# A routed expert's down product as one plain float32 product instead of three split ones

## The chip, the core and the metric

The kernel runs on one core of one Trainium2 chip. The metric is the time of one execution on the device in microseconds (us). Three timed runs of the kernel before gave 2541.50, 2541.91 and 2543.68, so the median is 2541.91.

The engines are named as the profile names them: PE is the matrix engine (PEld its weight loads), DVE the vector engine, ACT the scalar engine, POOL the engine that here only issues indirect DMAs (gathers and scatters), and SP the engine whose queue issues the weight loads. SPq, ACTq and POOLq are these engines' queues. PEclk is the clock granted to PE as a share of its full speed.

## The reference, cut to what matters

The program is one layer with attention and a mixture of experts, followed by two further layers with a dense feed-forward. Everything is float32. The change touches the experts alone. There are 512 tokens of width 1024 and 64 experts with an inner width of 256; each token goes to 8 experts.

```python
def swiglu(x, w1, w3, w2):
    return (jax.nn.silu(x @ w1) * (x @ w3)) @ w2

def expert_block(args):
    e, toks, gs = args
    xb = t[toks]                                     # gather of up to 128 token rows
    return swiglu(xb, w1[e], w3[e], w2[e]) * gs[:, None]

routed = jax.ops.segment_sum(out, row_tok, num_segments=n_tok)
```

For one expert, w1 and w3 are 1024 x 256 and w2 is 256 x 1024: 1 MB each, so 3 MB for every expert.

## The kernel before, in words

**How float32 is multiplied.** A weight tile of 128 x 2048 float32 is split in two (`_K.split`, lines 217 to 224): ACT copies it to a reduced float32 type (`wh`, line 220) and DVE subtracts that copy from the raw tile (`wl`, line 221). The activations are split in the same way (`xet` for the tokens, `aet` for the inner activations). A product is then three matmuls, low by high, high by low, high by high (`_K.mm3`, lines 226 to 230). The adaptive-norm weights at the start of the program are the one place where PE multiplies raw float32 tiles (line 547).

**The weight stream.** `_Stream` (lines 71 to 178) holds a list of jobs, each a load of a raw tile (`wraw`, issued on SP at lines 110 and 112) and a flag that says whether the tile is split. `get` hands out the next job: it loads ahead up to `raw` jobs (`LR`, 8 in the expert loop), splits ahead up to `ahead` jobs (`LA`, 2), and returns the two halves, or the raw tile itself where the flag is false.

**The slots.** All large tiles come from one pool of 22 slots of 8 KB a partition (`slot`, line 198): raw tiles, `wh`, `wl`, `xet`, and the expert's output `eo`, two of which share a slot. A slot is given out again when its last user is done, the one that came free first being taken first. Who takes a slot waits for its last user, on whichever engine.

**The experts.** The 64 experts are ordered by how many tokens they have (`moe_units`, line 965). The first 32 run alone, three of them with a second block of rows; the last 32 run in pairs that share one block of 128 rows, 64 for each. So there are 67 down products in all. `moe_ops` sets the order of work: up of one expert, down of the expert before it, and so on. An up takes two jobs (half of w1 and w3 each, 24 matmuls on PE together), a down takes one (w2, 12 matmuls). Between them stand the transposes of the next tokens (`xet<-xg`, line 233) and of the inner activations (`act_t`, line 1398). A down's result is scaled by the gates into `eo`, one half by DVE (line 1415) and one by ACT (line 1413). POOL then adds it to `acc` in DRAM by an indirect DMA (line 1217). Each of these scatters waits until the one before has landed. A loop for overflowing experts (line 1552) stands behind the last expert; it has no turn in the profiled execution, but all engines meet at it.

The order on every engine is that of the program text. The last expert jobs are followed in the stream by the weights of the next layer (`plan_mla`, line 1713).

Of the kernel before, what the change touches and what calls it, by code (L numbers as in the profile page):

```python
# [11 lines left out]
F32 = mybir.dt.float32  # L12
F32R = mybir.dt.float32r
BF16 = mybir.dt.bfloat16
I32 = mybir.dt.int32
AF = mybir.ActivationFunctionType
# [16 lines left out]
FIX, PAIRS = 2, 16  # L33

CAPS = ((2, 128), (5, 192), (16, 128), (24, 96), (32, 80), (50, 64), (64, 48))
LR=8; LA=2; MOE_RAW=7
MORE=(5,6)
NR=3; RQ=3; RV=2
NF=7
# [141 lines left out]
class _K:  # L181
# [806 lines left out]
    def plan_moe(self):  # L988
        a = self.a
        kp = lambda w, k: w.rearrange("(k p) n -> p k n", k=k)  # L990
        wr, s1, s3 = kp(a["w_router"][0], 8), kp(a["ws1"][0], 8), kp(a["ws3"][0], 8)
        j = [([wr, s1[:, :, 0:128]], True), ([s1[:, :, 128:256], s3[:, :, 0:128]], True),
             (s3[:, :, 128:256], True)]
        units = self.moe_units()
        regs = {}

        def weight(nms, k, r, ks):
            def f():
                if r < FIX:
                    v = [a[nm][0, r].rearrange("(p k) n -> p k n", k=k)[:, ks] for nm in nms]  # L1000
                else:
                    if r not in regs:
                        regs[r] = self.nc.sync.value_load(self.perm[0:1, r:r + 1], min_val=0, max_val=NE - 1)
                    v = [a[nm][0, bass.ds(regs[r], 1)].rearrange("e (p k) n -> p (e k) n", k=k)[:, ks] for nm in nms]
                return v if len(v) > 1 else v[0]
            return f() if r < FIX else f
        ops = self.moe_ops()
        for i, (op, u, m) in enumerate(ops):
            r = units[u][0][m]
            if op == "up":  # L1010
                j += [(weight(("w1", "w3"), 8, r, slice(4 * h, 4 * h + 4)), True) for h in range(2)]
                if i == 1:
                    j.append((kp(a["ws2"][0], 2), True))
            else:
                j.append((weight(("w2",), 2, r, slice(0, 2)), True))
        return j

    def moe_begin(self, hT):
# [67 lines left out]
    def moe_block(self, hT, h2d, x1d):  # L1086
        nc, V, a, st = self.nc, self.nc.vector, self.a, self.st
# [128 lines left out]
        def scatter(o, idx):  # L1216
            nc.gpsimd.indirect_dma_start(out=acc, out_offset=IndirectOffsetOnAxis(ap=idx, axis=0),  # L1217
                                         in_=o, in_offset=None, compute_op=OP.add)
# [158 lines left out]
        def xpose(x):  # L1377
            t = self.slot(F32R, "xet")
            xv = x.rearrange("p (d k) -> p k d", k=8)
            for j in range(2):  # L1380
                self.trs(t[:, j * 512:j * 512 + 512].rearrange("p (a b) -> p a b", b=128),
                         t[:, 1024 + j * 512:1536 + j * 512].rearrange("p (a b) -> p a b", b=128),
                         [xv[:, 4 * j + i] for i in range(4)])
            r = lambda t: t.rearrange("p (a b) -> p a b", b=128)
            return r(t[:, :1024]), r(t[:, 1024:])

        def up(ps, xT, w, half):

            o = ps.rearrange("p (m n) -> p m n", m=2)
            for kk in range(4):  # L1390
                kc = 4 * half + kk
                self.mm3(o, (xT[0][:, kc], xT[1][:, kc]), (w[0][:, :, kk], w[1][:, :, kk]), kc == 0, kc == 7)
# [4 lines left out]

        def act_t(sg):
            av = sg[:, 256:].rearrange("p (f k) -> p k f", k=2)
            t = self.small.tile([128, 512], F32R, name="aet", bufs=4)  # L1400
            r = lambda t: t.rearrange("p (a b) -> p a b", b=128)
            H, L = r(t[:, :256]), r(t[:, 256:])
            self.trs(H, L, [av[:, 0], av[:, 1]])
            return H, L

        def down(aT, w, gate, o, rows):
            for n in range(2):
                ps = self.ps()
                c = slice(n * 512, n * 512 + 512)
                for f in range(2):  # L1410
                    self.mm3(ps, (aT[0][:, f], aT[1][:, f]), (w[0][:, f, c], w[1][:, f, c]), f == 0, f == 1)
                if n:
                    nc.scalar.activation(o[rows, c], ps[rows], AF.Copy, scale=gate[rows])
                else:
                    V.tensor_scalar(o[rows, c], ps[rows], gate[rows], None, OP.mult)  # L1415
        first = [0]
        for _, nb in units:
            first.append(first[-1] + len(nb))
        st.raw, st.ahead = LR, LA
        ops = self.moe_ops()  # L1420
# [18 lines left out]
        def acts_t():  # L1439
            for u in ready:  # L1440
                aTs[u] = [act_t(sg) for sg in sgs.pop(u)]
            ready.clear()
# [57 lines left out]
        for i, (op, u, m) in enumerate(ops):  # L1500
# [13 lines left out]
            if op == "up":  # L1514
# [5 lines left out]
                w = st.get(True)  # L1520
# [4 lines left out]
                w = st.get(True)  # L1525
# [6 lines left out]
            else:  # L1532
                if u in ready:
                    acts_t()
                w = st.get()
                rows = slice(64 * m, 64 * m + 64) if len(ranks) > 1 else slice(0, 128)
                if m == 0:
                    outs[u] = []
                    for _ in nb:
                        if not half:  # L1540
                            t = self.slot(F32, "eo")
                            half.extend([t[:, 1024:], t[:, :1024]])
                        outs[u].append(half.pop())
                for b, n in enumerate(nb):
                    i = first[u] + b
                    down(aTs[u][b], w, gt[:, i:i + 1], outs[u][b], rows)
                    scatter(outs[u][b][rows][:n], (isc2 if m else isc)[:n, i:i + 1])
# [4 lines left out]
        with self.tc.For_i(0, nreg) as _:  # L1552
            ereg = nc.sync.value_load(li[0:1, 0:1], min_val=0, max_val=NE - 1)
            wt = []
            src = {nm: a[nm][0, bass.ds(ereg, 1)].rearrange("e (p k) n -> p (e k) n", k=k)
                   for nm, k in (("w1", 8), ("w3", 8), ("w2", 2))}
            for i in range(2):
                wv = self.slot(F32, f"ov_{i}")
# [4 lines left out]
            wv = self.slot(F32, "ov_w2")  # L1563
# [16 lines left out]
            ps = self.ps()  # L1580
# [8 lines left out]
            gt1 = self.sm([128, 1], "ov_gt", bufs=1)  # L1589
            c, cg = self.sm([128, 8, 3], "tc")[:, :1], self.sm([128, 8, 3], "tg")[:, :1]  # L1590
# [5 lines left out]
            xTe = xpose(xg(0))  # L1596

            H, L = self.slot(F32R, "wh"), self.slot(F32R, "wl")

            def wsplit(wv, how, **d):  # L1600
                self.split(H, L, wv)
                return H.rearrange(how, **d), L.rearrange(how, **d)
            ps = self.ps()
            for i in range(2):
                up(ps, xTe, wsplit(wt[i], "p (m k n) -> p m k n", m=2, n=256), i)
            sg = self.t2k("sg")
            act(sg, ps, slice(0, 128))
            aT = act_t(sg)
            o = wt[0][:, :1024]
            down(aT, wsplit(wt[2], "p (k n) -> p k n", k=2), gt1, o, slice(0, 128))  # L1610
            scatter(o, is1)
            l2 = self.t2k()[:, 0:3 * W + 3].rearrange("p (a b) -> p a b", b=W + 1)
            V.tensor_copy(l2, ll)
# [542 lines left out]
```

## Time and profile before

| | us |
|---|---|
| median of the timed runs | 2541.91 |
| the profiled execution, its own time | 2537.97 |
| its span, first to last instruction | 2536.2 |
| expert stage, from the first ups to the last down | 480 to 1215, 735 |
| PE busy in that stage | 667.51 |
| DVE busy in that stage | 620.79 |
| ACT busy in that stage | 488.03 |
| DMA engines busy in that stage | 0.96 of it, 324 GB/s |

The stage's numbers are from a view that gives each engine's busy time in a stretch. A matmul of 128 x 512 is recorded as busy for some 0.39 us but the next one starts 0.23 us after it, since matmuls are pipelined; so PE's pace is read from starts, not from durations. A DMA share is the mean over the core's 16 DMA engines, and can read a little over 1. Idle time that is ascribed to an engine which had long been done belongs to another cause, often a DMA.

### The profile page before, as it was taken

What the parts mean: (1) busy time and instruction counts of PE and PEld (TensorE: products, weight loads), DVE (VectorE), ACT (ScalarE), POOL (GpSimd) and SP (SyncE); (2) the same over time, 40 slices, a digit from 0 to 9 for tenths busy, and PEclk for the clock granted to TensorE, in tenths of its full rate; (3) what the DMA queues carried; (4) which work ended last, traced back from release to release, by engine and by line L of the source; (5) the groups of instructions that cost most, each with busy time, mean ns of one, the idle gap of its engine ahead of it and who ended that gap; (6) DMA issues with size and microseconds to landing.
All of it is one profiled execution on the core that took longest, in us unless ns stands there. A gap on an engine that the chain in (4) does not pass through costs nothing.

```text
span 2536.2 us, 30312 instructions
## 1 busy us (share of the span) xinstructions
PE 2308.6 (91%) x11356; PEld 1868.5 (74%) x11356; DVE 1604.4 (63%) x2569; ACT 1056.6 (42%) x1446; POOL 340.5 (13%) x184
## 2 busy tenths in 40 slices
PE   8877988798889899999599999999999998999998
PEld 4555767677767777777477788888788876888886
DVE  4599667697888888988576653333555667433335
ACT  2552433366657666777244222222234432322230
POOL 0642000133334323332100000000000000000000
PEclk9888999899989999999799999999999998999999
DMA  9443134699989999999311332332141121323310
GB/s 331 168 140 79 39 114 165 223 352 301 344 267 319 341 307 347 361 362 337 105 32 54 129 107 76 100 116 75 59 140 51 51 100 62 105 83 116 100 67 33
DMA packets 195014, 422.21 MB, mean 166 GB/s; under 512 B 21329, under 2 KB 99921, under 8 KB 186545
## 3 DMA queue, kind: packets, MB, share of 16 engines
q1 hardware_dynamic: 169984, 353.44, 39.8%
q0 software_dynamic: 12944, 39.20, 6.7%
q10 hardware_dynamic: 11938, 27.62, 3.0%
q8 instruction: 90, 1.47, 0.2%
q14 instruction: 58, 0.48, 0.1%
HBM read 390.78 MB, written 35.52 MB: 168 GB/s over the span
## 4 chain that ended last, share of the span: by engine, by line
PE 62%; DVE 20%; DMA 9%; ACT 4%; issue 4%; POOL 0%; ACTq 0%; DVEq 0%; SPq 0%; POOLq 0%
PE b L228 20%; PE b L229 19%; PE b L230 19%; DMA acc<-eo,isc 7%; DVE wl L221 6%; PE b L233 3%; ACT wh L220 2%; DVE work L754 1%; PE b L547 1%; DVE m L750 1%; DMA wraw<-in_w_ada_dram 1%; DVE ln_st L1643 1%; DVE work L732 1%; PE b L2029 1%; DVE eo L1415 1%
## 5 line engine op out<-in xcount | busy, mean ns | idle before, releaser
L221 DVE TENSOR_TENSOR wl<-wraw,wh 128x2048 fp32r<-128x2048 f32 (+2 forms) x311 | 701.7, 2264 | 397.5 <-ACT wh L220 328.9
L220 ACT ACTIVATE wh<-wraw 128x2048 fp32r<-128x2048 f32 (+2 forms) x311 | 584.4, 1887 | 181.0 <-DVE wl L221 62.1
L228 PE MATMUL b<-xtl,wh 128*128 128x512 f32 (+1 forms) x928 | 344.0, 371 | 2.9 <-DVE xtl L221 2.9
L229 PE MATMUL b<-xth,wl 128*128 128x512 f32 (+1 forms) x928 | 341.9, 368 | 0.0
L230 PE MATMUL b<-xth,wh 128*128 128x512 f32 (+1 forms) x928 | 341.8, 368 | 0.0
L228 PE MATMUL b<-wl,xet 128*128 128x512 f32 x536 | 222.4, 415 | 18.7 <-DVE wl L221 18.2
L1217 POOL DMA_INDIRECT acc<-eo,isc x67 | 155.2, 2316 | 485.0 <-DVE P L1151 123.5
L229 PE MATMUL b<-wh,xet 128*128 128x512 f32 x536 | 214.2, 400 | 2.2 <-DVE xet L221 2.2
L230 PE MATMUL b<-wh,xet 128*128 128x512 f32 x536 | 215.2, 401 | 0.0
L228 PEld LDWEIGHTS b<-xtl,wh 128*128 128x128 f32 x928 | 176.5, 190 | 32.7 <-DVE xtl L221 3.6
L230 PEld LDWEIGHTS b<-xth,wh 128*128 128x128 f32 x928 | 176.2, 190 | 28.8
L229 PEld LDWEIGHTS b<-xth,wl 128*128 128x128 f32 x928 | 176.4, 190 | 27.9
L228 PE MATMUL b<-wl,aet 128*128 128x512 f32 x268 | 117.1, 437 | 33.9 <-DVE wl L221 32.8
L228 PE MATMUL b<-wl,ath 128*128 128x512 f32 x352 | 139.3, 396 | 5.8 <-DVE wl L221 5.8
L230 PE MATMUL b<-wh,ath 128*128 128x512 f32 x352 | 138.6, 394 | 0.0
L229 PE MATMUL b<-wh,atl 128*128 128x512 f32 x352 | 138.6, 394 | 0.0
L926 ACT ACTIVATE p<-b,nm 128x128 f32<-128x128 f32 (+3 forms) x128 | 67.0, 526 | 166.2 <-DVE nm L923 127.1
L228 PEld LDWEIGHTS b<-wl,xet 128*128 128x128 f32 x536 | 104.0, 194 | 40.5 <-DVE wl L221 18.3
L230 PEld LDWEIGHTS b<-wh,xet 128*128 128x128 f32 x536 | 103.5, 193 | 23.6
L229 PEld LDWEIGHTS b<-wh,xet 128*128 128x128 f32 x536 | 103.9, 194 | 22.4 <-DVE xet L221 2.6
L229 PE MATMUL b<-wh,aet 128*128 128x512 f32 x268 | 113.0, 421 | 1.9 <-DVE aet L221 1.9
L230 PE MATMUL b<-wh,aet 128*128 128x512 f32 x268 | 111.1, 415 | 0.0
(461 smaller groups left out, 4342.0 us busy)
## 6 DMA issues: line engine op xcount, KB each, us to landing
wraw<-in_w_dram SPq DMA_DIRECT2D x256, 512.0 KB
wraw<-in_w_dram SPq DMA_DIRECT2D x64, 1024.0 KB
wraw<-in_ffn_w_gu_dram SPq DMA_DIRECT2D x44, 1024.0 KB
wraw<-in_w_ada_dram SPq DMA_DIRECT2D x24, 1024.0 KB
wraw<-in_ffn_w_down_dram SPq DMA_DIRECT2D x20, 1024.0 KB
wraw<-in_diff_w_in_dram SPq DMA_DIRECT2D x12, 1024.0 KB
wraw<-in_w_in_dram SPq DMA_DIRECT2D x8, 1024.0 KB
wraw<-in_w_in_dram SPq DMA_DIRECT2D x12, 512.0 KB
```

What stands on the lines that cost most here:

```text
L220: nc.scalar.activation(H, x, AF.Copy)
L221: nc.vector.tensor_tensor(out=L, in0=x, in1=H.bitcast(F32), op=OP.subtract)
L228: mm(ps, s[0], m[1], start=start, stop=False)
L229: mm(ps, s[1], m[0], start=False, stop=False)
L230: mm(ps, s[0], m[0], start=False, stop=stop)
L233: self.nc.tensor.transpose(ps, x, self.ident[:x.shape[0], :x.shape[0]])
L547: nc.tensor.matmul(ps, cb[:, kc, :], w[:, kk, :], start=False, stop=kc == 7)
L732: V.scalar_tensor_tensor(w, r[:, :nk], wi, w, op0=OP.mult, op1=OP.add)
L750: V.max(m8[qt - 1], work(qt))
L754: V.match_replace(work(qt), m8[qt - 1], work(qt), -3e38)
L926: nc.scalar.activation(p[:, :nk], ps[:, :nk], AF.Exp, bias=nm, accum_out=sm)
L1217: nc.gpsimd.indirect_dma_start(out=acc, out_offset=IndirectOffsetOnAxis(ap=idx, axis=0), in_=o, in_offset=None, compute_op=OP.add)
```

## The change

The jobs of w2 in the expert loop carry a false flag: the stream hands out the raw tile. `act_t` no longer splits the inner activations: it transposes into PSUM and ACT copies them once, as plain float32. `down` makes one plain float32 matmul of the raw tile for each of the four (column half, inner half) pairs, in place of three matmuls of split halves. `LR` is 9 in place of 8. The loop for overflowing experts is changed in the same way.

```diff
-LR=8; LA=2; MOE_RAW=7
+LR=9; LA=2; MOE_RAW=7
...
-                j.append((weight(("w2",), 2, r, slice(0, 2)), True))
+                j.append((weight(("w2",), 2, r, slice(0, 2)), None))
...
         def act_t(sg):
             av = sg[:, 256:].rearrange("p (f k) -> p k f", k=2)
-            t = self.small.tile([128, 512], F32R, name="aet", bufs=4)
-            r = lambda t: t.rearrange("p (a b) -> p a b", b=128)
-            H, L = r(t[:, :256]), r(t[:, 256:])
-            self.trs(H, L, [av[:, 0], av[:, 1]])
-            return H, L
+            t = self.small.tile([128, 256], F32, name="aet", bufs=4)
+            ps = self.ps()
+            for f in range(2):
+                self.tr(ps[:, f * 128:f * 128 + 128], av[:, f])
+            nc.scalar.activation(t, ps[:, :256], AF.Copy)
+            return t
...
                 for f in range(2):
-                    self.mm3(ps, (aT[0][:, f], aT[1][:, f]), (w[0][:, f, c], w[1][:, f, c]), f == 0, f == 1)
+                    nc.tensor.matmul(ps, aT[:, f * 128:f * 128 + 128], w[:, f, c], start=f == 0, stop=f == 1)
```

On PE, in the early part of the expert loop, stands before this: the transposes of the next tokens (`xg`), and then the down product of an expert (`wl` and `wh` are the halves of its w2, `aet` its activations), of whose twelve matmuls the first six are shown.

```order
L233 MATMUL b<-ident,xg 128x128 x8
L228 MATMUL b<-wl,aet 128x512
L229 MATMUL b<-wh,aet 128x512
L230 MATMUL b<-wh,aet 128x512
L228 MATMUL b<-wl,aet 128x512
L229 MATMUL b<-wh,aet 128x512
L230 MATMUL b<-wh,aet 128x512
```

And now, from the last matmul of the up before it to the token tables (`P`) behind it:

```order
L230 MATMUL b<-wh,xet 128x512
L233 MATMUL b<-ident,xg 128x128 x8
L1412 MATMUL b<-wraw,aet 128x512 x4
L1166 LDWEIGHTS P
L1166 MATMUL b<-idc,P 128x3
```

The twelve matmuls are four, at the same place in the order, and they read the raw tile.

On ACT, which copies the high halves, one pair of experts in the later part of the loop is this before (`xet` the next tokens, `sg` the inner activations, `eo` half of a down's result):

```order
L220 ACTIVATE wh<-wraw 128x2048 x2
L220 ACTIVATE xet<-b 128x512 x2
L1395 ACTIVATE sg<-b 64x256
L220 ACTIVATE wh<-wraw 128x2048
L1413 ACTIVATE eo<-b,gt 64x512
L220 ACTIVATE wh<-wraw 128x2048
L220 ACTIVATE aet<-b 128x256
L220 ACTIVATE wh<-wraw 128x2048
L1395 ACTIVATE sg<-b 64x256
L220 ACTIVATE wh<-wraw 128x2048
L1413 ACTIVATE eo<-b,gt 64x512
```

And now:

```order
L220 ACTIVATE wh<-wraw 128x2048
L220 ACTIVATE xet<-b 128x512 x2
L1395 ACTIVATE sg<-b 64x256
L220 ACTIVATE wh<-wraw 128x2048
L1414 ACTIVATE eo<-b,gt 64x512
L1404 ACTIVATE aet<-b 128x256
L220 ACTIVATE wh<-wraw 128x2048
L1395 ACTIVATE sg<-b 64x256
L220 ACTIVATE wh<-wraw 128x2048
L1414 ACTIVATE eo<-b,gt 64x512
```

Two of the pair's six copies are gone, and `aet` stands directly behind `eo`; on DVE the two `wl` that belong to them and `aet` are gone in the same way.

On SP, at the end of the expert loop, the loads of the next layer stand like this before, ahead of the overflow loop (`nov` is its count of turns):

```order
L110 DMA wraw<-in_mla_w_ukv_dram 128x512 x2
L110 DMA wraw<-in_mla_w_uq_dram 128x2x128 x3
L110 DMA wraw<-in_mla_w_ukv_dram 128x512 x2
L110 DMA wraw<-in_mla_w_uq_dram 128x2x128 x3
L110 DMA wraw<-in_mla_w_ukv_dram 128x512 x2
L1551 TENSOR_LOAD nov
```

And now:

```order
L110 DMA wraw<-in_mla_w_uq_dram 128x2x128 x3
L110 DMA wraw<-in_mla_w_ukv_dram 128x512 x2
L110 DMA wraw<-in_mla_w_uq_dram 128x2x128 x3
L110 DMA wraw<-in_mla_w_ukv_dram 128x512 x2
L1552 TENSOR_LOAD nov
```

One job of the next layer (three pieces of `w_uq` and two of `w_ukv`) stands behind the loop now, and behind the four loads of `acc` that follow it.

## Rows read from the trace of the kernel before

**Rows 1.** Busy time by stretch; the first row names the columns.

```profile
core 0: us, PE busy (x) PEld busy (x) DVE busy (x) ACT busy (x) POOL busy (x), PEclk, DMA share, GB/s
480.00:1215.00 735.00, 667.51 (x3290) 538.73 (x3291) 620.79 (x653) 488.03 (x476) 241.93 (x112) 0.95 0.96 324
1040.00:1160.00 120.00, 113.80 (x512) 90.69 (x510) 105.07 (x79) 91.34 (x80) 38.50 (x19) 1.00 1.02 365
610.00:620.00 10.00, 7.83 (x27) 6.34 (x28) 9.32 (x9) 6.08 (x8) 7.55 (x3) 0.62 0.63 122
740.00:750.00 10.00, 5.10 (x22) 3.70 (x22) 8.41 (x45) 0.00 (x0) 0.00 (x0) 0.52 0.37 91
```

**Rows 2.** Groups by line and form, 480 to 1215; busy and mean, then idle before.

```profile
L221 DVE TENSOR_TENSOR wl<-wraw,wh 128x2048 fp32r<-128x2048 f32 x191 | 435.4, 2287 | 89.2 <-ACT wh L220 63.0 <-issue 10.3 <-DMA acc<-eo,isc 5.7
...
L220 ACT ACTIVATE wh<-wraw 128x2048 fp32r<-128x2048 f32 x191 | 363.9, 1913 | 63.9 <-DMA acc<-eo,isc 48.4 <-DMA wraw<-in_w_dram 9.2 <-DMA x<-x1d 5.1
```

**Rows 3.** PE in order of time: two pairs of experts.

```profile
1024.31 1.04 PE L233 MATMUL b<-ident,xg 128*128 128x128 f32 x8
...
1063.15 1.04 PE L233 MATMUL b<-ident,xg 128*128 128x128 f32 x8
...
1081.33 1.04 PE L233 MATMUL b<-ident,xg 128*128 128x128 f32 x8
...
1084.00 0.50 PE L228 MATMUL b<-wl,aet 128*128 128x512 f32 x1 [1.63 <-DVE wl L221]
...
1086.90 0.40 PE L228 MATMUL b<-wl,xet 128*128 128x512 f32 x1
```

**Rows 4.** The plain products of line 547: order of time, then durations.

```profile
48.88 7.13 PE L547 MATMUL b<-wraw,g 128*128 128x512 f32 x16
...
L547 PE MATMUL b<-wraw,g x64: 592/592/1222, 7.7 to 55.4; 128*128 128x512 f32 x64
```

**Rows 5.** PE in order of time: stalls in the expert loop.

```profile
536.85 0.77 PE L228 MATMUL b<-wl,aet 128*128 128x512 f32 x1 [3.41 <-DVE wl L221]
...
612.17 0.80 PE L228 MATMUL b<-wl,xet 128*128 128x512 f32 x1 [7.87 <-DVE wl L221]
...
617.46 1.11 PE L233 MATMUL b<-ident,xg 128*128 128x128 f32 x8
...
1183.55 0.50 PE L228 MATMUL b<-wl,aet 128*128 128x512 f32 x1 [3.71 <-DVE wl L221]
```

**Rows 6.** The chain that ended last: what stood ahead of one stall.

```profile
596.24 11.41 DMA acc<-eo,isc
...
607.88 1.92 ACT wh L220
```

**Rows 7.** Waits, 480 to 1215: total, times, longest.

```profile
POOL acc L1217 <- DMA acc<-eo,isc: 114.5, 17, 10.4
...
ACT wh L220 <- DMA acc<-eo,isc: 48.4, 14, 7.2
...
ACT wh L220 <- DMA wraw<-in_w_dram: 9.2, 2, 8.7
```

**Rows 8.** Waits of SP's queue, 440 to 1215.

```profile
SPq L112 <- PE b L230: 165.6, 71, 12.4
```

**Rows 9.** POOL in order of time: scatters.

```profile
637.41 3.43 POOL L1217 DMA_INDIRECT acc<-eo,isc  x1 [6.89 <-DVE aet L221]
...
649.49 1.56 POOL L1217 DMA_INDIRECT acc<-eo,isc  x1 [5.47 <-DMA acc<-eo,isc]
...
1223.87 1.41 POOL L1217 DMA_INDIRECT acc<-eo,isc  x1 [4.55 <-DMA acc<-eo,isc]
```

**Rows 10.** Around the loop's end: ACT, then SP's loads, then ACT.

```profile
1215.94 0.69 ACT L1413 ACTIVATE eo<-b,gt 128x512 f32<-128x512 f32 x1 [3.48 <-PE b L230]
...
1267.32 1.41 SPq L110 DMA_DIRECT2D wraw<-in_mla_w_uq_dram  x3
...
1311.35 1.69 ACT L220 ACTIVATE wh<-wraw 128x1792 fp32r<-128x1792 f32 x1
```

More of the change, by code (lines that the diff above doesn't have):

```diff
@@ L1598, in moe_block @@
             H, L = self.slot(F32R, "wh"), self.slot(F32R, "wl")
-            def wsplit(wv, how, **d):
-                self.split(H, L, wv)
-                return H.rearrange(how, **d), L.rearrange(how, **d)
+            four = lambda t: t.rearrange("p (m k n) -> p m k n", m=2, n=256)
             ps = self.ps()
             for i in range(2):
-                up(ps, xTe, wsplit(wt[i], "p (m k n) -> p m k n", m=2, n=256), i)
+                self.split(H, L, wt[i])
+                up(ps, xTe, (four(H), four(L)), i)
             sg = self.t2k("sg")
@@ L1609, in moe_block @@
             o = wt[0][:, :1024]
-            down(aT, wsplit(wt[2], "p (k n) -> p k n", k=2), gt1, o, slice(0, 128))
+            down(aT, wt[2].rearrange("p (k n) -> p k n", k=2), gt1, o, slice(0, 128))
             scatter(o, is1)
```

## The prediction, made before the change was run

> **What bounds the kernel now.** I read the busy time by stretch first, since the change touches one stage only, the experts from 480 to 1215. Look there for what is nearly full: PE 667.5 of 735 us, DVE 620.8, the DMA engines at a share of 0.96 [rows 1]. Three things are close to full at once, so the sum has to be made against each of them.
>
> The DMA engines. In a smooth stretch, 1040 to 1160, their share reads 1.02; this is full. At that share the stage's transfers, which the change leaves as they are, would take 735 x 0.96 / 1.02 = 692 us. The DMA floor is thus 43 us under today's stage. Those 43 us are stretches such as 610 to 620 (share 0.63) and 740 to 750 (0.37) [rows 1].
>
> PE. The order of time shows its pace. Two pairs of experts take 1063.15 - 1024.31 = 38.8 us, 19.4 for a pair, while the next pair, from its transposes at 1063.15 to the next ones at 1081.33, runs with no real gap in 18.2 [rows 3]. So PE stands still for about 1.2 us in a pair, and the DMA engines, not PE, set the pair's pace.
>
> What makes PE stand still. At 612.17 an up has waited 7.87 us for a low half (`wl`) [rows 5]. The chain of waits says what is behind it: a scatter that took 11.41 us, then ACT's copy `wh` [rows 6]. ACT waited because the slot it had to write into was an `eo` that the scatter was still reading. ACT lost 48.4 us to such scatters in 14 waits, and 9.2 us to weights that had not landed [rows 7]. So the hold-ups come from slots, not from late loads. SP's loads too wait mainly for PE to give slots back, 165.6 us on line 230's matmuls alone [rows 8]. While PE stands, no slots come free, no loads start, and the DMA engines run dry: this is the share of 0.63 right behind the stall.
>
> **The change part by part.** The sum is made against the profiled execution (2537.97 us: a span of 2536.2 and 1.8 around it), which lies 3.9 under the median of the runs; differences carry over to that median.
>
> PE's products. A down has 12 matmuls, from 1084.00 to 1086.90, 2.90 us with a start-up of some 0.1, so 2.80 of pace [rows 3]. The plain product is in the trace with the same shape at line 547: 16 records, two passes for each of 8 products, in 7.13 us, the last of them 0.592 long [rows 4]. The pace is (7.13 - 0.592) / 15 = 0.436 us a pass, 0.872 a product. Four products are 3.49 us, against 2.80: +0.70 for a down. With 67 downs PE gets 47 us more work. A paired cycle without gaps grows from 18.2 to 19.6 us, which is 0.2 over today's 19.4: in the pairs PE becomes about as tight as the DMA engines are.
>
> The splits. 64 of the 192 splits of weight tiles go. DVE loses 64 x 2.287 = 146 us, ACT 64 x 1.913 = 122 [rows 2], and DVE also the low half of each `aet`. Neither engine is full, so none of this counts by itself; it counts where PE waited for `wl`, and there the cause was mostly a slot.
>
> The slots. A lone expert took three raw tiles, three `wh`, three `wl`, one `xet` and half an `eo`: 10.5 slots. Now it is 8.5. The pool of 22 goes round in 22 / 8.5 = 2.6 experts instead of 2.1; at 735 / 64 = 11.5 us for an expert, an `eo` is asked for again between 5 and 6 us later. That is near the size of the waits for scatters (48.4 / 14 = 3.5 us on average, 7.2 at most) [rows 7], so I expect most of them to go. What is late next is PE itself.
>
> PE's room. PE was idle for 735 - 667.5 = 67.5 us [rows 1]. Behind each long stall its clock is low as well: the up from 612.17 to 617.46 took 5.29 us in place of about 2.8, at a granted clock of 0.62 in that stretch [rows 1, 5]. I count 13 such places, the first at 536.85 and the last at 1183.55, with 1.7 to 2.5 us lost in each, some 24 us. Together 92 us are PE's to gain, and 735 - 92 + 47 = 690 is its new floor. Two losses do not hang on slots: the overflow tables around 740 to 750, where PE is busy for 5.10 of 10 us [rows 1], 5 us; and the last experts, where 3.71 us at 1183.55 [rows 5] and some 1.7 of slow matmuls behind it come from the loop running out, with an estimated 5 to 6 at the entry, where PE waits for the tables: 11 together. So PE's real floor is 706, above the DMA floor of 692.
>
> The ninth load is worth little: what holds a load back is a slot. Its bounds are 0 and the 3 us that 1 MB takes at 324 GB/s [rows 1]; I take 0. The `w2` raw tile is now held until its product is done, but two tiles fewer are held beside it.
>
> The loop's end. One job of the next layer moves on SP's queue past the overflow loop and the loads of `acc`. The next such job was issued at 1267.32 anyway, and the moved one is first wanted by ACT's copy at 1311.35 [rows 10]: 44 us of cover, so nothing. The last down is 0.7 us longer, but its scatter started at 1223.87, seven us behind the `eo` that it writes (1215.94 + 0.69), since scatters stand in line [rows 9, 10]: nothing again.
>
> The sum. Today's stage lies 43 us over its highest floor. With slots that come round a quarter later I keep 17 of the 43: 706 + 17 = 723, so 12 us less. With 5 to 25 kept, the forecast's own range is -24 to -4. On the profiled run it gives 2526, on the median **2530 us**.
>
> **A rule that is weighed.** For PE, the rows above show no gap in 18.2 of 19.4 us. The Trainium skill ("Perfetto Trace Analysis", Identifying the Most-Contended Engine) says to judge the matrix engine's room by the busy share of its weight loads rather than of its matmuls. By that rule 538.7 of 735 [rows 1], 73%, leaves more than a quarter free: the 47 us would cost nothing and the DMA floor would be the end, 43 us less. The rows speak against it: in a gapless stretch the starts set the pace. This is the last rival below.
>
> **The rivals.**
> *PE becomes the bound and the stalls stay (slower).* If PE's waits are not mostly slots, for instance because scatters simply take 11 to 12 us however many slots there are and `eo` piles up one expert later, then the idle stays and each down adds its 0.70 us. It decides at 47 of the 92 us: more idle left than that and the kernel is slower. With two thirds left (61 us) it is 14 us slower, 2556; with all, 47 slower. For it: pairs have only 1.2 us of idle to pay for 1.4. Against it: the waits of ACT for slots [rows 7], and DVE and ACT off the path.
> *The scatters set the pace (no change).* Scatters run one behind another: 637.41 to 649.49 is 12.1 us for one, started by the end of the one before [rows 9], and POOL waited 114.5 us for earlier scatters in 17 waits [rows 7]. A lone expert takes about that long today. If this chain is the bound, freeing slots only moves the wait; the lone experts keep their time and the pairs lose 16 x 0.2 = 3 us: 2545. For it: the rows named. Against it: most of POOL's waits are ascribed to other engines, though some of these had long been done.
> *PE has room after all (much faster).* 43 us less, 2499.
> That the ninth load does nothing is already in the forecast.
>
> **How the numbers follow.** Forecast 0.53, slower by PE 0.21, scatter chain 0.21, PE with room 0.05. A measurement of this kernel can tell 0.2%, 5 us, from no change. Faster by more than that: nearly all of the forecast (0.50), the last rival, and a quarter of the scatter chain, 0.60. Slower: nearly all of the first rival, 0.20. Within 0.2%: the rest, 0.20. The range that should hold 8 in 10 takes in the forecast's own (2518 to 2538), the scatter chain and the first rival up to its 2556 less a little, and leaves out the last: 2514 to 2554.
>
> **What the new profile would show.** The down as eight records at 0.44 us, 3.5 us in all; if they come at 0.6 or more, the product's price is wrong. ACT's waits for scatters well under 48 us. DVE some 450 to 470 us busy in the stage, ACT some 365. PE over 690 of about 723, DMA at 0.97 or more. The paired cycle at 19.6 to 19.9 us. If that cycle is 20.5 or longer, or if lone experts still stall PE for several us at a time, the forecast fails: the first means that PE is the bound with its own gaps, the second that slots were not the cause.

## The result: 31 us less, and the profile after

| | before | after |
|---|---|---|
| median of 4 runs each, us | 2541.70 | 2510.73 (2508.23 to 2514.89) |
| ratio, 95% interval | 1 | 0.9884 [0.9868, 0.9901] |
| profiled execution, its span, us | 2537.97, 2536.2 | 2514.89, 2513.1 |
| first to last down product, start to start, us | 707.4 | 689.6 |
| last down product to the next layer's first transposes, us | 25.4 | 21.7 |

The forecast of 2530 was right in sign; the time lies 3 us under its range. The two profiled executions differ by 23 us, since that of before lies 4 under its median and that of after 4 over. The expert stretch gives 18 of the 23, the stage's tail some 4.

Busy time by stretch in the changed kernel (columns as in [rows 1]):

```profile
480.00:1215.00 735.00, 687.05 (x3026) 479.60 (x3027) 471.53 (x542) 375.92 (x414) 183.81 (x114) 0.97 0.95 325
1040.00:1160.00 120.00, 120.00 (x466) 82.75 (x465) 80.83 (x64) 69.39 (x69) 27.64 (x18) 1.00 1.00 354
```

PE is now without a gap in the smooth stretch, where it stood still for 6 us before [rows 1]. DVE and ACT are busy for 149 and 112 us less (the prediction took off 146 and 122, and `aet`). In the smooth stretch the weight loads' share is 69% while the matmuls leave no room, so the rule on the weight loads' share (the prediction's last rival) does not hold here; e6 below puts a number to it.

Groups of the changed kernel, by line and form; busy time, mean of one in ns, then the idle time before:

```profile
L221 DVE TENSOR_TENSOR wl<-wraw,wh 128x2048 fp32r<-128x2048 f32 x127 | 290.9, 2291 | 201.2 <-ACT wh L220 197.8 <-issue 2.7
...
L220 ACT ACTIVATE wh<-wraw 128x2048 fp32r<-128x2048 f32 x127 | 242.8, 1913 | 44.3 <-DMA acc<-eo,isc 36.1 <-PE b L233 5.2 <-DMA wraw<-in_w_dram 1.6
...
L1217 POOL DMA_INDIRECT acc<-eo,isc x67 | 106.5, 1590 | 524.2 <-DVE P L1151 105.6 <-DMA acc<-eo,isc 94.0 <-DVE eo L1416 92.0
```

A split takes as long as before [rows 2], but DVE now waits for ACT's copies for 198 us; before it was 63. DVE now stands ready before its input is. The scatters were not part of the change, and yet POOL issues one in 1590 ns; over the kernel before it took 2316 on average (last section).

PE in order of time, a pair of experts of the changed kernel:

```profile
1087.23 1.04 PE L233 MATMUL b<-ident,xg 128*128 128x128 f32 x8
1088.11 3.60 PE L1412 MATMUL b<-wraw,aet 128*128 128x512 f32 x8
...
1091.78 0.40 PE L229 MATMUL b<-wh,xet 128*128 128x512 f32 x1
...
1106.21 1.04 PE L233 MATMUL b<-ident,xg 128*128 128x128 f32 x8
```

A pair takes 1106.21 - 1087.23 = 18.98 us; the prediction said 19.6 to 19.9. The waits, 480 to 1215, in total, times and longest:

```profile
POOL acc L1217 <- DMA acc<-eo,isc: 94.0, 14, 8.3
...
ACT wh L220 <- DMA acc<-eo,isc: 36.1, 7, 8.4
PE b L228 <- DVE wl L221: 18.0, 11, 5.9
```

ACT's waits for scatters are half as many, but longer, 5.2 us on average against 3.5: 36 us are left of 48 [rows 7]. PE's waits for `wl` fell to 18.0 us in 11 waits. In the kernel before they were:

```profile
PE b L228 <- DVE wl L221: 51.0, 24, 7.9
```

The largest that is left is of the old kind. The chain ahead of it, in order of time, and then PE at its end:

```profile
620.28 10.81 DMA acc<-eo,isc
...
631.24 1.92 ACT wh L220
...
633.18 2.30 DVE wl L221
...
635.62 0.77 PE b L228
```

```profile
635.62 0.77 PE L228 MATMUL b<-wl,xet 128*128 128x512 f32 x1 [5.90 <-DVE wl L221]
```

A scatter lands 10.81 us after its issue, ACT gets its tile, and PE waits 5.90 us, as in [rows 5, 6].

### The profile page after: what moved, and what is told of

It is laid out like the page before. It is cut to its first block, busy times and chain, and to the rows that moved or that the text cites. A ratio compares the mean times of both kernels' runs of the same rounds, so it can differ in the third digit from the quotient of the medians.

```text
span 2513.1 us, 29500 instructions
## 1 busy us (share of the span) xinstructions
PE 2324.9 (93%) x11088; PEld 1806.3 (72%) x11088; DVE 1450.4 (58%) x2454; ACT 941.6 (37%) x1382; POOL 277.9 (11%) x184
## 4 chain that ended last, share of the span: by engine, by line
PE 71%; DVE 16%; DMA 5%; ACT 4%; issue 2%; POOL 1%; ACTq 0%; DVEq 0%; POOLq 0%; SPq 0%
PE b L228 20%; PE b L230 19%; PE b L229 19%; PE b L1412 7%; DMA acc<-eo,isc 4%; PE b L233 4%; DVE wl L221 4%; ACT wh L220 2%; DVE work L754 1%; PE b L547 1%; DVE m L750 1%; DMA wraw<-in_w_ada_dram 1%; DVE ln_st L1642 1%; POOL p L659 1%; PE b L2028 1%
## 5 line engine op out<-in xcount | busy, mean ns | idle before, releaser
L221 DVE TENSOR_TENSOR wl<-wraw,wh 128x2048 fp32r<-128x2048 f32 (+2 forms) x247 | 557.4, 2261 | 507.1 <-ACT wh L220 461.2
L220 ACT ACTIVATE wh<-wraw 128x2048 fp32r<-128x2048 f32 (+2 forms) x247 | 463.3, 1880 | 159.9 <-DVE wl L221 62.6
L228 PE MATMUL b<-wl,xet 128*128 128x512 f32 x536 | 231.0, 431 | 18.1 <-DVE wl L221 18.0
L1412 PE MATMUL b<-wraw,aet 128*128 128x512 f32 x536 | 242.2, 596 | 0.8 <-ACT aet L1404 0.8
L1412 PEld LDWEIGHTS b<-wraw,aet 128*128 128x128 f32 x536 | 99.0, 191 | 101.7 <-issue 96.9
L1217 POOL DMA_INDIRECT acc<-eo,isc x67 | 106.5, 1590 | 524.2 <-DVE P L1151 105.6
L1933 ACT ACTIVATE t2k<-b 128x512 f32<-128x512 f32 x44 | 26.3, 598 | 185.9 <-PE b L230 185.9
```

The lines of the kernel that those rows point to most:

```text
L220: nc.scalar.activation(H, x, AF.Copy)
L221: nc.vector.tensor_tensor(out=L, in0=x, in1=H.bitcast(F32), op=OP.subtract)
L228: mm(ps, s[0], m[1], start=start, stop=False)
L1412: nc.tensor.matmul(ps, aT[:, f * 128:f * 128 + 128], w[:, f, c], start=f == 0, stop=f == 1)
L1933: nc.scalar.activation(sg, pss[j], AF.Silu)
```

## A ledger for the experiments

For each profile I took the time from the start of the first down product to that of the last ("stretch" in the table, in us). It is cut into steps, from one down product to the next. The shortest that each step took in any of the kernels with PE's work of before add up to 629 us, in those with the plain product to 663.5. What a kernel has above its sum I call **lost**; it holds everything that PE had to wait for, whatever the cause. A single profile has some us of chance in it; the verdict on a time is the ratio, from all runs (0.1% is 2.5 us).

| run | edit | ratio to before, 95% | stretch | lost |
|---|---|---|---|---|
| | before | 1 | 707 | 78 |
| | after | 0.9884 [0.9868, 0.9901] | 690 | 26 |
| e1 | after, 3 tiles held | 0.9943 [0.9921, 0.9966] | 709 | 46 |
| e2 | after, splits and their tiles kept | 1.0050 [1.0029, 1.0071] | 723 | 60 |
| e3 | after, splits into one spare tile | 0.9940 [0.9919, 0.9961] | 698 | 35 |
| e4 | before, 1/4 of w2's splits | 0.9875 [0.9851, 0.9899] | 680 | 51 |
| e7 | before, 1/4 of DVE's part only | 0.9867 [0.9846, 0.9889] | 681 | 52 |
| e8 | before, no scatters | 0.9674 [0.9659, 0.9690] | 642 | 13 |
| e9 | after, no scatters | 0.9761 [0.9739, 0.9783] | 667 | 4 |
| e5 | after, 3 of 4 products | 0.9838 [0.9818, 0.9858] | 666 | 59 |
| e6 | after, 5 products | 1.0042 [1.0028, 1.0056] | 726 | 6 |
| e10 | after, two sums | 0.9865 [0.9844, 0.9886] | 667 | 3 |
| e11 | before, two sums | 0.9998 [0.9987, 1.0010] | 695 | 66 |
| e13 | e10, zeroed early | 0.9853 [0.9832, 0.9874] | 670 | 6 |
| e14 | e13, lone experts split | 0.9971 [0.9958, 0.9984] | 690 | 48 |
| e15 | e7 and two sums | 0.9871 [0.9849, 0.9893] | 669 | 40 |
| e12 | after, 8 loads | 0.9849 [0.9827, 0.9871] | 679 | 16 |
| e16 | before, 9 loads | 1.0099 [1.0080, 1.0118] | 731 | 102 |
| e17 | after, 7 loads | 0.9860 [0.9834, 0.9885] | 670 | 6 |
| e18 | e13, 8 loads | 0.9844 [0.9822, 0.9866] | 668 | 5 |

For e5 and e6 the sum is moved by 66 x 0.86 us, since 66 down products lie in the stretch; for e14 by some 21. Differences in us between two runs are taken from their ratios.

## Experiments: tiles or work?

**e1**, three tiles taken out of the pool:

```diff
         ops = self.moe_ops()
+        held = [self.slot(F32, "held") for _ in range(3)]
+        for t in held:
+            nc.vector.memset(t[:, 0:1], 0.0)
```

> The changed kernel with three of its 22 big tiles taken out of the pool from the start of the routed experts to their end (one column of each is written and read, nothing else); loads, splits and products stay as changed. Theory A (the gain came from tiles that come free sooner): the pool goes round in about 2.2 experts again, the stalls of PE of the kernel before come back on top of the dearer down product, and most of the 65 us (31 us net and 34 us that the product costs) is lost: 2555 to 2575 us, PE idle in the expert stretch about twice the 40 us of after. Theory B (the gain came from the splits that DVE and ACT no longer do): three tiles fewer cost little, 2508 to 2520 us.

**e2**, w2 split into two tiles that only wait for the product:

```diff
-                j.append((weight(("w2",), 2, r, slice(0, 2)), None))
+                j.append((weight(("w2",), 2, r, slice(0, 2)), "both"))
...
-                w = st.get()
+                w, wH, wL = st.get()
...
+                V.tensor_copy(dummy, wH[:, 0:1].bitcast(F32))
+                V.tensor_copy(dummy, wL[:, 0:1].bitcast(F32))
```

> The changed kernel with its plain down product, but w2 is still split by ACT and DVE into two further tiles, which nothing but a read of one column after the down product uses: the dearer product together with the old work and the old tiles (the raw tile lives longer than in the kernel before, up to the product). Theory A and theory B alike: the price of the product without its gain, 2541 + 34 = 2575 us, 2565 to 2590; a time near 2511 would say that neither the tiles nor the work matter and the product itself brought the gain. The three parts told apart: the difference to the run with three tiles held is what the splits' work is worth when tiles are short.

**e3**, the same splits into one spare tile (in `_split`):

```diff
+        elif self.junk is not None:
+            t, n, v = self.rawt[i]
+            self.k.split(self.junk, self.junk2, t)
...
+        st.junk = self.slot(F32, "junk")
+        st.junk2 = st.junk
```

> The changed kernel, with every w2 tile still split by ACT and DVE at the place of the kernel before, but into one tile that is set apart for it: ACT and DVE do the old work, while the tiles of the pool are only one fewer. Theory A: the work lies beside PE, one tile fewer costs 3 to 8 us: 2513 to 2522 us. Theory B: the 65 us go back for the most part: 2550 to 2575 us. POOL's scatters, which took 2316 ns to issue before and 1590 ns after, go back towards 2300 ns if DVE's work is what slowed them.

**e4** and **e7**, relief in the kernel before: e4 splits 512 of w2's 2048 columns on both engines; in e7 DVE alone is spared:

```diff
-            self.k.split(H[:, :n], L[:, :n], t[:, :n])
+            if kind == "part":
+                self.k.nc.scalar.activation(H[:, :n], t[:, :n], AF.Copy)
+                self.k.nc.vector.tensor_tensor(out=L[:, :512], in0=t[:, :512], in1=H[:, :512].bitcast(F32), op=OP.subtract)
```

> The kernel before, but of every w2 tile ACT and DVE split only the first 512 of 2048 columns, and all three-part down products read these (the output of the routed experts is wrong by that): three quarters of the splits' work for w2 is gone, some 105 us of DVE and 90 us of ACT, while the tiles taken and PE's instructions stay as they were. Theory A: tiles come free a little sooner only through the shorter split, 2530 to 2541 us. Theory B: DVE and ACT were what PE waited for: most of the 65 us come, 2480 to 2500 us.

> The kernel before; of every w2 tile ACT still rounds all 2048 columns, DVE subtracts only the first 512, and all three-part down products read these columns (output wrong by that): the relief of DVE alone, tiles and PE's instructions as before. With the relief of both engines 32 us came. If DVE's time is what counts (through PE's waits for wl and POOL's longer scatters): 2508 to 2518 us, and POOL's issue near 1750 ns. If ACT's time is what counts, 2530 us or more; if both, about 2520 us.

Neither theory held as a whole; only e3's median, 2521 us, lies in a range, that of theory A. Three tiles fewer cost 15 us (0.9943 against 0.9884), the old work with one tile fewer 14, both together 42. And in the kernel before, relief alone, without one tile or product changed, brought 32 us, and relief of DVE alone as much, 34. I had forecast 0 to 11 for it by theory A. Work and tiles thus both count, and they are not a sum: the work is worth 27 (e2 against e1) to 34 us (e7) where tiles are scarce and under 14 (e3) where they are not.

How missing tiles cost time is not what theory A said, though. With three tiles held, ACT hardly waits for scatters; it waits for weights that have landed late (e1, 480 to 1215):

```profile
ACT wh L220 <- DMA wraw<-in_w_dram: 56.4, 21, 16.3
...
ACT wh L220 <- DMA acc<-eo,isc: 0.8, 1, 0.8
```

In the changed kernel the first of these lines reads 1.6 us, 3 times.

Why DVE? The waits of e7, 480 to 1215, in total, times and longest:

```profile
ACT wh L122 <- DMA acc<-eo,isc: 61.5, 15, 10.5
...
PE b L232 <- DVE wl L123: 21.1, 11, 7.6
PE b L232 <- DVE wl L225: 14.3, 20, 2.9
```

The scatters hold ACT up no less than before, 61.5 us in 15 waits against 48.4 in 14; but PE waits for `wl` 35 us and not 51. The cause of the stalls is there unchanged, and less of it gets through to PE. A relieved DVE makes up for part of it. (A shorter subtraction, 0.69 us in place of 2.29, also gives the raw tile back some 1.6 us sooner; no run takes the two apart.)

## Experiments: without the scatters

**e8** and **e9** leave out the 67 scatters, in the kernel before and in the changed one:

```diff
                     down(aTs[u][b], w, gt[:, i:i + 1], outs[u][b], rows)
-                    scatter(outs[u][b][rows][:n], (isc2 if m else isc)[:n, i:i + 1])
```

> The kernel before without the 67 scatters of the routed experts' results (the output lacks these experts): the tiles of results come free as soon as they are written, and POOL has 155 us less to do. If the chain of scatters that add up behind each other holds the tiles and with them the loads and splits: the 48 us for which ACT waits for scatters go, and 2500 to 2515 us. If it lies beside the other work: 2530 to 2541 us (the stage's end alone, 15 us of trailing scatters, comes back in either case).

> The changed kernel without the 67 scatters of the routed experts' results (the output lacks these experts), beside the same edit of the kernel before, which took 2459 us. Theory S (the tiles and the work of DVE that the change gives back are worth something only because a chain of scatters holds tiles): without scatters nothing is gained and the dearer product is paid, 34 us more than 2459: 2480 to 2495 us. Theory A (tiles and work are worth their 65 us in any case): 2459 - 31, 2425 to 2435 us.

The kernel before gets 83 us faster, far more than forecast, the changed one only 31, and without scatters **the change makes the kernel slower by 22 us** (0.9674 to 0.9761; the medians are 2458.9 and 2481.6). So theory S: without scatters what the change gives back is worth less than PE's dearer product, and it pays only because of them. Leaving them out takes away three things at once: the hold on tiles, POOL's issues, and the bytes that they move (from rate and stretch, an estimated 211 MB are left of 233). Which of them makes up the 83 us, e8 can't tell; for the changed kernel the two sums below settle it. The stretch 600 to 700 of three kernels shows how little room is left. The kernel before:

```profile
600.00:700.00 100.00, 83.04 (x428) 67.02 (x427) 78.49 (x85) 62.56 (x65) 41.43 (x18) 0.91 0.98 321
```

The same without scatters:

```profile
600.00:700.00 100.00, 99.28 (x555) 81.37 (x554) 99.10 (x108) 77.58 (x79) 18.79 (x11) 1.00 0.98 340
```

The changed kernel without scatters:

```profile
600.00:700.00 100.00, 100.00 (x493) 70.68 (x493) 74.58 (x87) 57.82 (x68) 14.93 (x11) 1.00 0.94 320
```

Left alone, the kernel before runs PE at 99.3% and DVE at 99.1% in this stretch of lone experts: at PE's full pace **DVE is just as full**. Little stalls as long as nothing disturbs it (13 us lost in e8). My reading, which e7 bears out: each time that a scatter holds ACT's tile, DVE falls behind, and as it has no spare time it can't catch up, so that PE pays for the wait. The 78% that DVE showed before was a DVE that was being held up. In the changed kernel DVE is busy for 75% of the time at PE's full pace, so it can make up a quarter of the time that passes.

Two runs change PE's pace alone. **e5** leaves out one product of four, **e6** does one twice:

```diff
-                for f in range(2):
+                for f in (0, 1) if n else (0,):
...
-                for f in range(2):
+                for s, f in enumerate((0, 1) if n else (0, 1, 1)):
```

> The changed kernel with three of the four plain products of each down product (the output of the routed experts is wrong by that): 0.87 us of PE less per down product, 67 x 0.87 = 58 us in all, tiles and splits as changed. Theory P (after the change PE sets the pace of the expert stretch): nearly all of it comes, 2455 to 2470 us. Theory D (the loads' floor of 692 us lies just under PE's): 15 to 25 us come and then the loads hold it, 2485 to 2497 us.

> The changed kernel with one of the four plain products of each down product done twice (the output is wrong by that): 58 us of PE more. Theory P: all of it is paid, 2565 to 2572 us. If some other chain (loads, scatters) sets the pace after the change, less than two thirds of it: under 2550 us.

12 us of 58 came back and 40 of 58 were paid. Theory P fails on both sides: with a faster PE more is lost (59 us), with a slower one nearly nothing (6). Theory D forecast 15 to 25 us for e5 (its range holds the median, 2496.5), and the trace speaks for it in part: from the first down product to the last the DMA engines' share is 1.00 at 350 GB/s (0.98 at 330 in the kernel before), and e15 (below) is like it. First e5, then e15:

```profile
504.25:1169.71 665.46, 620.97 (x2788) 444.23 (x2786) 449.81 (x513) 362.01 (x404) 199.47 (x110) 0.96 1.00 350
```

```profile
508.88:1177.96 669.08, 630.42 (x3185) 509.20 (x3183) 506.59 (x623) 476.65 (x466) 177.68 (x110) 0.98 1.00 349
```

Both take 666 to 670 us, though PE's sum would allow 607 and 629. So do e10, e13, e17 and e18, but there PE's sum is 663.5. No kernel with scatters takes less. In e5 ACT also waits for weights that landed late, 18.6 us against 1.6 in the changed kernel, and still 45.6 us for scatters. So some of what is lost in these two may be the loads' own floor and not DVE or the tiles; no run separates them.

## Experiments: two sums, and the loads

**e10** and **e11**: the scatters go in turn to two sums (e10 of after, e11 of before; the second is set to zero first and added at the end). **e13** does the zeroing some 80 us earlier:

```diff
-                    scatter(outs[u][b][rows][:n], (isc2 if m else isc)[:n, i:i + 1])
+                    scatter(outs[u][b][rows][:n], (isc2 if m else isc)[:n, i:i + 1], (acc, self.acc2)[i % 2])
...
+            V.tensor_tensor(out=E(tt), in0=E(tt), in1=E2(tt), op=OP.add)
```

> The changed kernel; its scatters go in turn to two sums in DRAM, the second set to zero before the routed experts and added to the first after them (four loads and four additions more, some 8 us): a scatter waits for the last but one, not for the last. If the serial chain is what holds the tiles, most of PE's 40 us of stalls go: 2480 to 2500 us. If the length of one scatter holds them, or POOL's issue, 2510 us or a little more.

> The kernel before with the same two sums. Without scatters 83 us came; if the serial chain brings most of that: 2470 to 2500 us, and as PE's three-part product is cheaper it would then beat the changed kernel with two sums. If the chain is not it: 2530 to 2550 us.

> The changed kernel with two sums, the second set to zero some 80 us earlier, where the DMA engines are nearly idle; in the first run with two sums the zeroing held up a weight load, and the first down product came 10 us late. The expert stretch had no stall left there (666.9 us from the first down product to the last, against 689.6 of the changed kernel). If the 10 us come back in full: 2495 to 2500 us. If another load is late instead: 2505 us.

In the changed kernel two sums take the rest of the stalls away (3 us lost), though as many bytes are scattered: ACT's waits for scatters fall from 36.1 us to 3.3 in e10. So there it was the chain. PE in the stretch 600 to 700 of e13:

```profile
600.00:700.00 100.00, 100.00 (x489) 71.74 (x488) 71.72 (x81) 58.15 (x69) 26.30 (x21) 1.00 1.03 344
```

Of that gain the zeroing and the adding eat most: 8 us come for e13 (intervals that just overlap). In the kernel before two sums bring nothing (e11), and ACT's waits for scatters don't get shorter there, 56.4 us in 16 against 48.4 in 14. Why not is open: the full DVE would be a reason, but e15 below, with DVE relieved, still has 54 us of them. Two more runs mix the parts. **e14** is e13 with the three-part product for the lone experts, which cost PE less and DVE 35 splits more; **e15** is e7 with two sums:

```diff
-                    down(aTs[u][b], w, gt[:, i:i + 1], outs[u][b], rows)
+                    (down if len(units[u][0]) > 1 else down3)(aTs[u][b], w, gt[:, i:i + 1], outs[u][b], rows)
```

> The same, but for the units of one expert (35 of the 67 down products) w2 and its activations are split again and multiplied in three parts: 0.6 us of PE less for each, 21 us in all, against 35 more splits on DVE and ACT and two more tiles for each. If PE alone sets the pace once the chain is halved: about 20 us less than the run before it, 2475 to 2480 us. If DVE's spare time is what absorbs the scatters: no gain or a loss, 2495 to 2515 us.

> The kernel before with the relief of DVE (it subtracts 512 of w2's 2048 columns, output wrong by that) and with two sums: the relief alone brought 34 us, two sums alone some 7 us in the expert stretch. If the two work on one and the same wait (a scatter holds a tile, and DVE has to make up for it afterwards): together more than their sum, PE's floor of 629 us nearly reached: 2465 to 2480 us. If they are separate: about 2500 us.

e14 is 30 us slower than e13, a larger loss than forecast: more splits and two tiles more for each lone expert cost far more than the 21 us of PE that they save. e15 brings nothing over e7 in time (0.9871 and 0.9867); its stretch is 12 us shorter, against a dearer entry and end. That the two would add up to more than their sum was wrong; tiles are as scarce in e15 as before, and its DMA engines' share is 1.00.

**e12, e16, e17, e18** set the number of loads ahead, all by one line:

```diff
-LR=9; LA=2; MOE_RAW=7
+LR=8; LA=2; MOE_RAW=7
```

> The changed kernel with eight loads ahead, not nine. The prediction held the ninth load for nothing: 2508 to 2515 us. If the tiles that came free are worth something only as loads further ahead: 2520 us or more.

> The kernel before with nine loads ahead: the ninth load alone, where tiles are scarcer still. With the rest of the change it cost 9 us. If one more load ahead takes a tile that the splits or the results would need: 2545 to 2560 us; if it is nothing here, 2538 to 2545 us.

> The changed kernel with seven loads ahead. Eight were 9 us better than nine. If a tile that waits loaded is always worth more elsewhere: 2493 to 2500 us. If seven is too few to ride out a late load (an expert takes three loads, so seven are 2.3 experts): 2503 to 2515 us.

> The changed kernel with eight loads ahead and two sums, set to zero early. Each alone brought 8 to 9 us. If both cure the same wait for scatters, no more than 3 us come on top, since the stretch with two sums (669.9 us) has only 6 us left above the 663.5 of stall-free cycles: 2496 to 2502 us. If they cure different waits: 2490 to 2495 us.

**The ninth load is a loss**: 26 us on the kernel before, and about 9 with the rest of the change, where I had expected none or a gain (the intervals of e12 and after meet at 0.987). It takes a tile that a result would have had. Waits of the kernel before with nine loads, 480 to 1215:

```profile
ACT eo L1413 <- DMA acc<-eo,isc: 60.9, 12, 9.4
...
DVE eo L1415 <- DMA acc<-eo,isc: 29.8, 11, 6.2
```

With eight loads these two are 10.7 us in 2 waits and 4.3 in 2. SP's waits with nine loads, 480 to 1240:

```profile
SPq L112 <- DVE wl L221: 178.3, 73, 10.9
```

With eight SP waited 101.5 us in 33 times for DVE to give a tile back: the load that runs further ahead stands in line for the very tiles that DVE is late with. In e12 ACT has no wait for an expert's scatter left at all (DVE has two, 9.5 us). Seven loads are as good as eight, and two sums on top of eight add nothing. So the change of the down product alone, at eight loads, is worth 38 us (0.9849), and the ninth load gives 9 of it back. Eight loads with the plain product, 2501.6 us, beat both kernels, and of the kernels that do all of the work none was faster by more than its interval.

## Why the prediction was right in sign and 19 us too high

- **PE's products** (+0.70 for a down, 47 us): the right mechanism, mis-sized. The down takes 3.44 us at 0.43 a pass, as said. But the pair of before "with no real gap in 18.2" holds a stop. Where the second down of the pair begins, its starts are 0.43, 0.37 and 0.33 us apart in place of 0.23, since DVE has the `wl` of its w2 done at 1070.36 + 2.29 = 1072.65 only, and the low half of `aet` after that. The subtraction, and then PE:

```profile
1070.36 2.29 DVE L221 TENSOR_TENSOR wl<-wraw,wh 128x2048 fp32r<-128x2048 f32 x1
```

```profile
1072.37 0.39 PE L230 MATMUL b<-wh,xet 128*128 128x512 f32 x1
1072.80 0.47 PE L228 MATMUL b<-wl,aet 128*128 128x512 f32 x1
1073.17 0.50 PE L229 MATMUL b<-wh,aet 128*128 128x512 f32 x1
1073.50 0.39 PE L230 MATMUL b<-wh,aet 128*128 128x512 f32 x1
```

  With DVE relieved (e7) the stop is gone and the same pair takes 1060.51 - 1042.77 = 17.74 us; without scatters, DVE busy for 95% of the pair, it is there again, 1025.67 - 1007.49 = 18.18. First e7, then e8, PE in order of time:

```profile
1042.77 1.04 PE L237 MATMUL b<-ident,xg 128*128 128x128 f32 x8
...
1060.51 1.04 PE L237 MATMUL b<-ident,xg 128*128 128x128 f32 x8
```

```profile
1007.49 1.04 PE L233 MATMUL b<-ident,xg 128*128 128x128 f32 x8
...
1025.67 1.04 PE L233 MATMUL b<-ident,xg 128*128 128x128 f32 x8
```

  So PE's price is (18.98 - 17.74) / 2 = 0.62 for a down, 42 us in all, and against the 18.18 with the stop only 0.40 of it shows. (The ledger's two sums differ by 34, since some steps have a wait left in every kernel with three-part products.)
- **The splits: "none of this counts by itself". This is the step that failed.** It judged DVE by its share of a stretch that has stalls in it (621 of 735). Relief of DVE alone was worth 34 us (e7) where the prediction put nothing. e3 shows the same from the other side: it gives back the tiles but one and keeps the old work, and is 15 us faster than the kernel before, near the 12 that were forecast from tiles; the rest of the 31 comes with the work (and the one tile). The right sum could be made from the trace of before. DVE there in order of time:

```profile
636.78 0.42 DVE L221 TENSOR_TENSOR aet<-b,aet 128x256 fp32r<-128x256 f32 x1
637.12 2.28 DVE L221 TENSOR_TENSOR wl<-wraw,wh 128x2048 fp32r<-128x2048 f32 x1
639.31 1.28 DVE L221 TENSOR_TENSOR xet<-b,xet 128x512 fp32r<-128x512 f32 x2
640.51 0.41 DVE L1396 TENSOR_TENSOR sg<-sg,b 128x256 f32<-128x256 f32 x1
640.85 2.29 DVE L221 TENSOR_TENSOR wl<-wraw,wh 128x2048 fp32r<-128x2048 f32 x1
```

  From start to start a lone expert asks DVE for 3 x 2.19 (splits) + 1.20 (`xet`) + 0.34 (`aet`) + 0.34 (`sg`), and 0.66 for its half of `eo` and some 0.6 for a mask `P`: 9.7 us. PE's shortest step for a lone expert is 9.7 as well. One split less makes it 7.2 of 10.35 (`aet` goes too).
- **The slots**: right that they matter and that scatters are behind the stalls. But that most of ACT's waits would go was too much (48 to 36 us), and three tiles given back cost 15 us, not all. The prediction's own sign against it, lone experts that still stall PE for several us, is there: 5.90 us at 635.62.
- **The ninth load: 0, bounds 0 and 3 us of gain.** Wrong: a loss of about 9, and 26 alone. The prediction saw that tiles hold the loads back, and missed that a load ahead takes a tile too.
- **What stays of the friction** (17 of 43 us kept): too much, as DVE's spare time was not in it.
- **The floor of the loads** (692 us for the stage, from a share of 1.02 read as full): a share near 1 doesn't say how much can be moved. From 1040 to 1160 e7 moves 373 GB/s at the same share, against 365 [rows 1]. That the engines are nearly full was right, and it may be what counts once PE has less to do (e5, e15).
- **The rivals.** PE as the bound came half true: e6 shows that 40 of 58 us of more PE work would be paid now, and e5 that only 12 would come back. The scatter chain was rightly named as the source, but not as a pace that no change can move. PE's room is refuted for the most part by the same 40 of 58; that its 2499 us lie nearer to the measured time than the forecast is chance.
- **The end of the loop**: nothing there became later; the tail is 4 us shorter.

What stays open: how the 34 us of e7 divide between DVE's catching up, raw tiles that come free sooner, and POOL's shorter issues (below). No run separates them; that e12 loses less than the changed kernel although its scatters take 1965 ns to issue speaks against the last.

## What to carry over

Work out each engine's demand at the pace of the fastest one, not its share of the stalled span: here two engines were both nearly full at that pace, and relief of the one that showed 78% was worth 34 us. A loads-ahead count is paid from the same pool as everything else; test it alone, in both directions. A dearer instruction on the engine that waits can make the faster kernel, if it takes work from the one that it waits for.

## What the runs showed of the hardware

POOL's issue of a scatter is longer beside DVE's subtractions. In the kernel before 59 of 65 issues lay beside a subtraction `wl<-wraw,wh` for more than 0.05 us and took 2.44 us on average, the other 6 took 1.42; in the changed kernel 30 took 1.75 and 37 took 1.46, none of these 37 more than 1.62 (worked out from the order of time of both engines). A long issue also has more chance to lie beside something, so two runs that change the work count for more. With DVE alone relieved (e7) the mean is 1559 ns, with the old splits put back on both engines (e3) it is 2237 again. First e7, then e3, 480 to 1215:

```profile
L1221 POOL DMA_INDIRECT acc<-eo,isc x67 | 104.5, 1559 | 519.6 <-DMA acc<-eo,isc 168.7 <-DVE wl L123 118.1 <-DVE P L1155 109.1
```

```profile
L1221 POOL DMA_INDIRECT acc<-eo,isc x67 | 149.9, 2237 | 479.5 <-DVE eo L1420 68.9 <-DMA acc<-eo,isc 63.7 <-ACT wh L224 43.5
```

DVE's own time for a split does not change (2287 ns before, 2291 after). The amount of subtraction is not all: e12 splits no more than the changed kernel and has 1965 ns. The Trainium skill ("SBUF — State Buffer", Who interferes with whom) says that a DVE instruction with two inputs in SBUF contends with a GpSimd instruction that reads SBUF. The longer issues beside subtractions would fit that; what an issue reads, no trace here shows.

The second sum's zeros (2.6 MB, in ten writes) held up what stood behind them on SP's queue: in e10 the writes are issued from 344.71 to 351.55, and the loads of `x` behind them (not of weights, as e13's expectation has it) at 351.66 in place of 345.70. PE was busy for 9.80 us of 340 to 360 in place of 17.30, and the first down product came 10 us later. Written early they delay it by 3 to 6.
